# Sums of weight quarters: on VectorE, or by accumulating transfers

## The chip, the cores and the metric

The kernel runs on one core of a Trainium2 chip. A core has TensorE (matrix products into PSUM banks), VectorE and ScalarE (elementwise work), GpSimd (POOL in the profile) and SyncE (SP), each an engine with an in-order queue of its own, and 16 DMA engines that they share. The metric is the device time of one execution in microseconds: less is better.

## The reference

One inference step of a decoder of two layers, for a prompt of 1024 tokens and 8 single sample tokens, which the kernel handles together as 1032 columns. Layer 0 mixes tokens by a gated linear recurrence, layer 1 by a wide causal convolution. In both, a cross-attention over 256 memory tokens and then a gated feed-forward block follow. Only the last is touched:

```
gu = h @ ffn_w_up[i]                 # (1032, 1024) @ (1024, 6144)
g, u = gu[..., :3072], gu[..., 3072:]
g = causal depthwise convolution of width 3 over g (+ bias)
out = (gelu(g) * u) @ ffn_w_down[i]
```

All of it is float32.

## The kernel before, in words

*Precision.* Every operand of a matmul is split in a high part h, rounded by ScalarE (`act`), and a low part l, the rest, subtracted by VectorE. A product is three passes: hh, hl, lh.

*The up projection, seven products for eight.* The 24 gate tiles of 128 outputs and the 24 value tiles are taken in pairs p. Of a pair, the weights are two tiles of 128 x 8 x 128 (one of the gate, one of the value), each in two halves of the contraction: four quarters A11, A12 (gate), A21, A22 (value) of 128 x 512 floats. The activations are also cut in four (two halves of the contraction, two halves of the columns). A product of 2 x 2 blocks takes eight block products; the kernel uses the scheme of Strassen and Winograd with seven, P1 to P7, whose operands are sums and differences of the quarters. `QP` says for each product which of three PSUM accumulators (a, b, c) it goes into and which activation operand (b11, b21, b22, t1 to t4) it uses; `QFIRST`, `qsequence` and `QLAST` write out the order of the 168 products of a layer, in the middle P1, P6, P2, P7, P5, P4, P3 of one pair after the other.

*Weights.* Three products use a quarter as it is (P1: A11, P2: A12, P4: A22). The other four use sums, which class `QWeights` (from L587) makes on VectorE in tiles `ws`: (1) A21 + A22, (2) that minus A11, (3) A11 - A21, (4) A12 minus sum 2. `high` and `low` split the result in `wh` and `wl`. The two tiles of a pair are loaded whole, 512 KB each, by SP through `load_raw` into a ring of three buffers `w`; `fetch` issues the next load once all readers of the oldest tile stand in the program.

*The loop over products* (in `ffn`, from L1267). In iteration i TensorE runs product i (`qprod`, L521: four k-blocks, three passes, two chunks of 258 columns, 24 matmuls), then the program gives ScalarE `high(i + 5)` and VectorE `low(i + 4)`, the next steps of the convolution of earlier pairs (`conv`; one of them is a GpSimd copy of the last columns of g into `fstash`), the evacuation of product i (`evac`), the weight sums that a table `wsums` puts in this iteration, and what `beside` adds for the activations of the first nine iterations. Products that share an accumulator wait for the evacuation between them: P1 is copied out of a (tile e) before P2 is added in it, P6 out of b (tile g) before P7, P7 (tile u) before P4, P5 out of c before P3. Iterations 7, 9 and 10 hold the three parts of the row norms (`Rms`: matmuls with ones, a square root on ScalarE, a reciprocal on VectorE).

*Before the loop* the output projection of the attention (`out_proj`, from L826) makes eight output tiles of 72 matmuls each, and behind each of them parts of the first operands: at its tiles 5 and 6 the first four sums and the first weight splits. Tile 7 is computed before tile 6 is worked on. It reloads x from DRAM through SP and spills it through ScalarE's queue.

*After the loop* `close` releases the loads of the down projection, which uses the same ring `w` and DRAM copies `ad` of the gated activations.

Of the kernel before, what the change touches and what calls it, by code (L numbers as in the profile page):

```python
# [15 lines left out]
P = 128  # L16
D = 1024
KD = 8
# [29 lines left out]
NPART = 3  # L48
LOOK = 2
RAHEAD = 1  # L50


@with_exitstack
def hybrid_step(
# [70 lines left out]
    def f32(ap):  # L125
        return ap.bitcast(F32)
# [60 lines left out]
                w_cols((nme, l, m), w[l, 0, m])  # L187

    def w_ffn(l):
        for t in range(24):  # L190
            w_cols(("up", l, t), w_up[l, 0, t])
            w_cols(("up", l, 24 + t), w_up[l, 0, 24 + t])
        for gi in range(24 // GS):
            for m2 in range(4):
                w_cols(("dn", l, gi, m2), w_down[l, gi, m2], GS, 256)
# [36 lines left out]
    def prep(n):  # L232

        while wstate["made"] < min(wstate["cur"] + n, wstate["lim"]):
            i = wstate["made"]
            load_raw(i + 1 + RAHEAD)
            w = W(order[i][1])
            for j in range(2):
                act(w.h[j], wraw[i][:, j * w.n:(j + 1) * w.n])
            wmade.append(w)  # L240
            wstate["made"] += 1
        prep_low(n)
# [14 lines left out]
        wstate["cur"] += 1  # L257
        return wmade[i]

    limits = [i for i, o in enumerate(order) if o[0][0:1] == ("up",) and order[i - 1][0][0] == "o"]  # L260
    wstate["lim"] = limits.pop(0)


# [265 lines left out]
    class Quarters:  # L529
# [13 lines left out]
        def sum(self, n, i):  # L543

            y, t = self.y, self.t
            a, b, into = {"t1": (y.get((i, 1)), y.get((i, 0)), None),
                          "t2": (y.get((i + 2, 1)), t.get(("t1", i)), t.get(("t1", i))),
                          "t3": (y.get((i + 2, 1)), y.get((i, 1)), y.get((i, 1))),
                          "t4": (y.get((i + 2, 0)), t.get(("t2", i)), y.get((i + 2, 0)))}[n]
            t[(n, i)] = slot(n, [P, 2, HT]) if into is None else into  # L550
            tt(V, t[(n, i)], a, b, ALU.subtract)
# [5 lines left out]
        def high(self, n, i):  # L557
            h = self.ops[n][0]
            h[i] = slot(n + "h", [P, 2, HT], F32R)
            act(h[i], self.src(n, i))  # L560

        def low(self, n, i):
            h, l = self.ops[n]
            l[i] = slot(n + "l", [P, 2, HT], F32R)
            tt(V, l[i], self.src(n, i), f32(h[i]), ALU.subtract)

        def split(self, n, i):
            self.high(n, i)
# [18 lines left out]
    class QWeights:  # L587


        SUM = {"P5": 1, "P6": 2, "P7": 3, "P3": 4}  # L590

        def __init__(self, pairs, seq):
            self.pairs, self.seq = pairs, seq
            self.sums, self.made, self.slots = {}, {}, {}

        def start(self, base):
            self.base = base
            for p, (k0, k1) in enumerate(self.pairs):
                assert (order[base + 2 * p][0], order[base + 2 * p + 1][0]) == (k0, k1)

            self.left = {base + 2 * p + i: 7 - 2 * i for p in range(len(self.pairs)) for i in range(2)}
            self.done = base

        def fetch(self):

            while self.left.get(self.done) == 0:
                self.done += 1
            load_raw(min(self.done + NRAW, self.base + 2 * len(self.pairs)))

        def raw(self, p, i, half):  # L610
            n = self.base + 2 * p + i
            load_raw(n + 1)
            self.left[n] -= 1
            assert self.left[n] >= 0
            return wraw[n][:, 4 * half:4 * half + 4, :]

        def sum(self, p, n):
            if (p, n) in self.sums or p >= len(self.pairs):
                return
            half = (p, n > 2)  # L620
            if half not in self.slots:
                self.slots[half] = slot("ws", [P, 2, 4, P])
            t = self.slots[half][:, (n - 1) % 2]
            op = ALU.subtract
            if n == 1:
                a, b, op = self.raw(p, 1, 0), self.raw(p, 1, 1), ALU.add
            elif n == 2:
                a, b = self.sums[(p, 1)], self.raw(p, 0, 0)
            elif n == 3:
                a, b = self.raw(p, 0, 0), self.raw(p, 1, 0)  # L630
            else:
                a, b = self.raw(p, 0, 1), self.sums[(p, 2)]
            self.sums[(p, n)] = t
            tt(V, t, a, b, op)

        def src(self, n):
            p, name = self.seq[n]
            if name in self.SUM:
                return self.sums[(p, self.SUM[name])]
            return self.raw(p, *{"P1": (0, 0), "P2": (0, 1), "P4": (1, 1)}[name])  # L640

        def high(self, n):
            if n < len(self.seq):
# [7 lines left out]
                tt(V, w[1], self.src(n), f32(w[0]), ALU.subtract)  # L651

        def close(self):
            n = 2 * len(self.pairs)
            for key in ("cur", "made", "low"):
                wstate[key] = self.base + n
            wmade.extend([None] * (self.base + n - len(wmade)))
            wstate["lim"] = len(order) if not limits else limits.pop(0)

    st = {}  # L660
# [165 lines left out]
    def out_proj(key, ops, g, src, dst, done=(), hooks={}, pair=None, quarters=None, qw=None):  # L826
# [13 lines left out]
        for m in range(KD):  # L840
            if m < len(done) and done[m] is not None:
                ps = done[m]
            else:
                ps = mmt()
                step(ps, getw(key + (m,)), ops, hooks.get(m))
            xm = xs[m]
            tt(V, v3(xm), ps[:, :, 0:CH], v3(xm), ALU.add)
            if quarters:
                quarters.tile(m, xm, g(m))
                norm_tile(st, m, xm, None, m > 5)  # L850
            else:
                xg.append(norm_tile(st, m, xm, g(m)))
            spill(dst, m, xm)
            if m + 2 < KD:
                xs.append(reload(src, m + 2))
            if not quarters:
                continue
            if m in (1, 3):
                quarters.sum("t1", m // 2)
                quarters.high("b11", m // 2)  # L860
            if m in (2, 4):
                quarters.low("b11", m // 2 - 1)
                quarters.split("t1", m // 2 - 1)
            if m == 5:
                qw.fetch()
                for n in range(1, 5):
                    qw.sum(0, n)
                qw.high(0)
                qw.low(0)
                quarters.sum("t2", 0)  # L870
                quarters.split("b21", 0)
            if m == 6:

                late = mmt()
                step(late, getw(key + (7,)), ops, hooks.get(7))
                done = [None] * 7 + [late]
                for n in range(1, 4):
                    qw.high(n)
                    qw.low(n)
                qw.fetch()  # L880
                quarters.high("t2", 0)
            if m == 7:
                quarters.low("t2", 0)
                quarters.sum("t2", 1)
                quarters.split("b21", 1)
# [21 lines left out]
        G.dma_start(out=o_lru_conv_s[0, :, 0:2, :], in_=state_lru_conv[0, :, 1:3, :])  # L907


    up_w = [QWeights([(("up", l, t), ("up", l, 24 + t)) for t in range(24)], qsequence(24)) for l in range(2)]  # L910
    pm = const([P, 2, NS, 32], "pm")
    G.memset(pm, 0.0)

    def attention(l, st, xg, g_next, src, dst, hooks=None):
        qw = up_w[l]
        qw.start(wstate["cur"] + 2 * KD)
        qd = dram([NS, NH, HD], f"qd{l}")
        od = dram([4, P, NP], f"od{l}")
        q, q8, o = {}, {}, {}
# [347 lines left out]
    def ffn(l, st, q, g_next, src, dst, hooks={}):  # L1267
# [12 lines left out]
        def evac(p, n):  # L1280
# [5 lines left out]
            elif n == "P6":  # L1286
                if p not in gs:
                    gs[p] = slot("g")
                tt(V, hv(gs[p][:, hi]), ps, hv(es[p]), ALU.add)
            elif n == "P2":  # L1290
                if p not in gs:
                    gs[p] = slot("g")
                act(hv(gs[p][:, lo]), ps)
            elif n == "P7":
                us[p] = slot("u")
                tt(V, hv(us[p][:, hi]), ps, hv(es[p]), ALU.add)
                if p in left:
                    left.pop(p)()
            elif n == "P5":
# [4 lines left out]
                else:  # L1304
                    left[p] = fin
            elif n == "P4":
                tt(V, hv(us[p][:, lo]), ps, hv(es.pop(p)), ALU.add)
            elif n == "P3":
                tt(V, hv(gs[p][:, hi]), ps, hv(gs[p][:, hi]), ALU.add)

        whole = {p: i for i, (p, n) in enumerate(seq) if n == "P3"}

# [35 lines left out]
        def a_parts(t):  # L1348
            parts[t] = parts_of("act", raw.pop(t))


        wsums = {0: [(1, 1), (1, 2)], 2: [(1, 3)], 4: [(1, 4)], 9: [(2, 1), (2, 2)], 11: [(2, 3)], 13: [(2, 4)]}
        for i, (p, n) in enumerate(seq):
            if p > 1 and i > 14 and n in ("P2", "P7", "P5"):
                if p == npair - 2:
                    wsums[i - 1 if n == "P2" else i] = {"P2": [(p + 1, 1)], "P7": [(p + 1, 2)], "P5": [(p + 1, 3)]}[n]
                    wsums[i + 1] = [(p + 1, 4)] if n == "P5" else []
                    continue
                wsums[i] = {"P2": [(p + 1, 1), (p + 1, 2)], "P7": [(p + 1, 3)], "P5": [(p + 1, 4)]}[n]
        r = Rms(st["acc"], *st["late"])  # L1360
        PART = {7: 0, 9: 1, 10: 2}
        end = len(seq) - len(QP)
# [1 line left out]
        for i, (p, n) in enumerate(seq):  # L1364
# [22 lines left out]
            conv(i)  # L1387
            if s <= 3:
                evac(p, n)
            for k in wsums.get(i, ()):  # L1390
                qw.sum(*k)
            qw.fetch()
            for f, *at in beside.get(i, ()):
                f(*at)
        use_banks("mm")
# [449 lines left out]
```

## Time and profile before

| | |
|---|---|
| median of 3 runs | 2850.26 us (2848.57 to 2850.32) |
| the profiled execution, whole | 2849.45 us |
| its span in the trace | 2847.3 us |
| TensorE busy | 2799.0 us (98%), 19814 matmuls |
| VectorE busy | 1887.3 us (66%) |
| ScalarE busy | 1082.9 us (38%) |
| GpSimd busy | 95.8 us (3%) |
| DMA: SP's queue, ScalarE's, GpSimd's | 249.45, 52.82 and 19.07 MB |
| HBM read, written | 255.25 and 67.23 MB |

The two up projections lie about from 645 to 1138 us and from 2061 to 2554 us. The granted clock of TensorE is at its full level nearly throughout (0.998 on the mean). A busy share says how long an engine had work; whether that work decides the time is read from who waits for whom.

### The profile page before, as it was taken

To read this page: it belongs to the slowest core of one execution; us is meant where nothing else is said; L and a number is where in the kernel's file an instruction comes from. 1 tells how busy PE (TensorE), PEld (TensorE's weight loads), DVE (VectorE), ACT (ScalarE), POOL (GpSimd) and SP (SyncE) were. 2 spreads that over 40 slices of the span, in tenths; PEclk is the share of its full clock that TensorE was granted. 3 is DMA by queue.
4 is the path that set the end of the run, shared out by engine and by line. 5 is a ranking of instruction groups with operands and counts; after the bars stand their busy time and mean duration, and the time that the engine had idled before them with its cause. 6 is when DMAs were issued, how large, how long until landed. Compare 5 with 4: busy or idle time off the path is not lost.

```text
span 2847.3 us, 46857 instructions
## 1 busy us (share of the span) xinstructions
PE 2799.0 (98%) x19814; PEld 2701.6 (95%) x19814; DVE 1887.3 (66%) x2673; ACT 1082.9 (38%) x1608; POOL 95.8 (3%) x175
## 2 busy tenths in 40 slices
PE   8999999999999999999999999999999999999998
PEld 6999999899999999999999679998999999999997
DVE  7686445658777777436688975456587777773456
ACT  7465333444333334322321154333453333343223
POOL 1000000000000000000000100000000000000001
PEclk9999999999999999999999999999999999999999
DMA  8111425732222223333312644267322222233231
GB/s 292 49 45 52 142 82 198 260 115 67 83 75 83 76 82 108 124 123 136 116 45 81 152 134 178 90 222 237 117 69 69 90 69 88 74 137 111 90 136 60
DMA packets 128529, 324.32 MB, mean 114 GB/s; under 512 B 17523, under 2 KB 61619, under 8 KB 128280
## 3 DMA queue, kind: packets, MB, share of 16 engines
q1 hardware_dynamic: 100976, 249.45, 27.0%
q10 hardware_dynamic: 15696, 52.82, 4.6%
q0 software_dynamic: 11648, 19.07, 2.5%
q8 instruction: 155, 2.54, 0.4%
q14 instruction: 54, 0.44, 0.0%
HBM read 255.25 MB, written 67.23 MB: 113 GB/s over the span
## 4 chain that ended last, share of the span: by engine, by line
PE 90%; DVE 4%; DMA 2%; ACT 2%; issue 1%; POOLq 0%; POOL 0%; ACTq 0%; DVEq 0%; SPq 0%
PE mm L277 48%; PE qm L521 33%; PE aux L1628 2%; PE mm L374 2%; PE aux L942 1%; DMA qb<-qd 1%; PE aux L985 1%; PE mm L1505 1%; PE aux L1505 1%; DMA w<-in_w_kv_dram 1%; DVE kc L120 1%; PE aux L461 1%; PE aux L1067 0%; DVE wl L117 0%; DVE qf L117 0%
## 5 line engine op out<-in xcount | busy, mean ns | idle before, releaser
L114 ACT ACTIVATE wh<-w 128x512 fp32r<-128x512 f32 x468 | 279.9, 624 | 461.5 <-PE mm L277 294.5
L117 DVE TENSOR_TENSOR wl<-w,wh 128x512 fp32r<-128x512 f32 x468 | 306.1, 686 | 106.4 <-ACT wh L114 106.4
L277 PE MATMUL mm<-xgh,wh 128*128 128x344 f32 x1152 | 249.0, 324 | 2.0 <-DVE qf L117 2.0
L277 PE MATMUL mm<-xgh,wl 128*128 128x344 f32 x1152 | 244.1, 320 | 0.0
L277 PE MATMUL mm<-xgl,wh 128*128 128x344 f32 x1152 | 244.1, 320 | 0.0
L277 PE MATMUL mm<-acth,wh 128*128 128x344 f32 x1056 | 223.8, 320 | 0.0
L277 PE MATMUL mm<-acth,wl 128*128 128x344 f32 x1056 | 223.8, 320 | 0.0
L277 PE MATMUL mm<-actl,wh 128*128 128x344 f32 x1056 | 223.8, 320 | 0.0
L277 PEld LDWEIGHTS mm<-xgh,wh 128*128 128x128 f32 x1152 | 190.8, 188 | 8.3 <-issue 3.3
L277 PEld LDWEIGHTS mm<-xgh,wl 128*128 128x128 f32 x1152 | 193.6, 188 | 0.0
L277 PEld LDWEIGHTS mm<-xgl,wh 128*128 128x128 f32 x1152 | 193.2, 188 | 0.0
L114 ACT ACTIVATE wh<-ws 128x512 fp32r<-128x512 f32 x192 | 120.8, 629 | 164.1 <-PE qm L521 133.4
L117 DVE TENSOR_TENSOR z<-mm,z 128x1032 f32<-128x1032 f32 x64 | 78.8, 1232 | 152.6 <-PE mm L277 152.6
L277 PEld LDWEIGHTS mm<-acth,wl 128*128 128x128 f32 x1056 | 177.6, 188 | 0.0
L277 PEld LDWEIGHTS mm<-actl,wh 128*128 128x128 f32 x1056 | 177.0, 188 | 0.0
L277 PEld LDWEIGHTS mm<-acth,wh 128*128 128x128 f32 x1056 | 176.7, 188 | 0.1
L120 DVE SCALAR_TENSOR_TENSOR dc<-glu,colB,dc 128x1015 f32<-128x1015 f32 (+29 forms) x120 | 145.9, 1265 | 0.7
L117 DVE TENSOR_TENSOR wl<-ws,wh 128x512 fp32r<-128x512 f32 x192 | 131.2, 684 | 7.7 <-ACT wh L114 7.7
L120 DVE SCALAR_TENSOR_TENSOR c<-g,colB,c 128x1023 f32<-128x1023 f32 x96 | 122.8, 1279 | 0.0
L117 DVE TENSOR_TENSOR x<-mm,x 128x1032 f32<-128x1032 f32 x40 | 49.3, 1232 | 108.4 <-PE mm L277 108.4
L117 DVE TENSOR_TENSOR acc<-acc,sq 128x1032 f32<-128x1032 f32 (+3 forms) x59 | 60.0, 1017 | 73.7 <-ACT sq L114 73.4
L117 DVE TENSOR_TENSOR g<-qm,e 128x516 f32<-128x516 f32 x48 | 33.4, 695 | 113.3 <-PE qm L521 113.3
(347 smaller groups left out, 6657.6 us busy)
## 6 DMA issues: line engine op xcount, KB each, us to landing
w<-in_w_up_dram SPq DMA_DIRECT2D x96, 512.0 KB, 3.6
ad<-u ACTq DMA_DIRECT2D x48, 516.0 KB, 2.7
ar<-ad SPq DMA_DIRECT2D x48, 516.0 KB, 4.7
w<-in_w_down_dram SPq DMA_DIRECT2D x48, 512.0 KB, 3.7
xd<-x ACTq DMA_DIRECT2D x40, 516.0 KB, 2.7
x<-xd SPq DMA_DIRECT2D x40, 516.0 KB, 5.4
w<-in_w_kv_dram SPq DMA_DIRECT2D x32, 512.0 KB, 5.1
kc<-in_cache_mem_k_dram SPq DMA_DIRECT2D x32, 512.0 KB, 7.6
```

The lines of the kernel that those rows point to most:

```text
L114: return S.activation(out=out, in_=in_, func=func, **kw)
L117: return e.tensor_tensor(out=out, in0=a, in1=b, op=op)
L120: return V.scalar_tensor_tensor(out=out, in0=a, scalar=sc, in1=b, op0=op0, op1=op1, **kw)
L277: PE.matmul(ps[:, c, 0:CH], w[wi](k), xs[k][xi][:, c * CH:(c + 1) * CH], start=(k == first and n == 0), stop=(k == last and n == passes[-1]))
L374: PE.matmul(ps[:, t, :], kv.memg[k // 4][xi][:, k % 4, t * P:(t + 1) * P], w[wi](k % 2), start=(k == 0 and n == 0), stop=(k == KD - 1 and ...
L461: PE.matmul(out, ident[:, 32 * g:32 * g + 1].to_broadcast([P, P]), self.q, start=True, stop=True)
L521: PE.matmul(acc[:, c, 0:HC], w[wi][:, k, :], x[xi][k // 2][:, k % 2, c * HC:(c + 1) * HC], start=first and k == 0 and i == 0, stop=last an ...
L942: PE.matmul(a[:, t * 256:(t + 1) * 256], q[2 * self.h + d][qi][:, c0:c0 + P], self.kv[ki][:, d * 256:(d + 1) * 256], start=(d == 0 and n = ...
L985: PE.matmul(a, self.kv[vi][:, c0:c0 + P], self.PT[hf][pi][:, mc, :], start=(mc == 0 and n == 0), stop=(mc == 1 and n == len(PASSES) - 1))
L1505: PE.matmul(ps[:, 0:n], w[m // 2][wi](k)[:, (m % 2) * P:(m % 2 + 1) * P], a[k][xi][:, r], start=(k == 0 and i == 0), stop=(k == GS - 1 and ...
L1628: PE.matmul(a[32 * g:32 * g + 32, lo:512], tap_w[j][:, 4 * q + g, :], tap_x[j][g][:, s0:s0 + 512 - lo], start=(q == 0), stop=(q == 7), til ...
```

## The change

Each product's weights now get a tile of their own, filled by transfers from DRAM: the first quarter plain from SP, each further quarter by a transfer from GpSimd that adds to what lies there (`accum_op`). `PARTS` lists the quarters of each product, 14 per pair, seven plain and seven added. Since only additions are made, the weight sums of P3, P6 (and P4's use of e) come with other signs than before: `t3` and `b22` are negated on the activations' side, P4, P6, P7 and P3 are evacuated with subtractions whose operands are swapped or whose operation changes. The four sums on VectorE, `fetch`, `raw` and the table `wsums` go, and the up weights leave the list `order` of whole tiles. `todo` gives part r of product n the iteration n - 7 - 2 x (parts - 1 - r), so that the last part is issued seven products ahead and parts lie two products apart; `go(i)` issues what is due, at the end of iteration i, and at output tiles 4, 5 and 6 before the loop. A tile holds two products; odd ones come from the general slots `ws`, the others from the ring `w`. `load_raw` in `prep` no longer reads past the limit.

```diff
+QAHEAD = 7
@@ w_ffn
-        for t in range(24):
-            w_cols(("up", l, t), w_up[l, 0, t])
-            w_cols(("up", l, 24 + t), w_up[l, 0, 24 + t])
@@ prep
-            load_raw(i + 1 + RAHEAD)
+            load_raw(min(i + 1 + RAHEAD, wstate["lim"]))
@@ Quarters
-                          "t3": (y.get((i + 2, 1)), y.get((i, 1)), y.get((i, 1))),
+                          "t3": (y.get((i, 1)), y.get((i + 2, 1)), y.get((i, 1))),
...
-            act(h[i], self.src(n, i))
+            act(h[i], self.src(n, i), **({"scale": -1.0} if n == "b22" else {}))
...
-            tt(V, l[i], self.src(n, i), f32(h[i]), ALU.subtract)
+            if n == "b22":
+                stt(l[i], self.src(n, i), -1.0, f32(h[i]), ALU.mult, ALU.subtract)
+            else:
+                tt(V, l[i], self.src(n, i), f32(h[i]), ALU.subtract)
@@ QWeights
-            if n == 1:
-                a, b, op = self.raw(p, 1, 0), self.raw(p, 1, 1), ALU.add
-            elif n == 2:
-                a, b = self.sums[(p, 1)], self.raw(p, 0, 0)
-            elif n == 3:
-                a, b = self.raw(p, 0, 0), self.raw(p, 1, 0)
-            else:
-                a, b = self.raw(p, 0, 1), self.sums[(p, 2)]
-            self.sums[(p, n)] = t
-            tt(V, t, a, b, op)
+        PARTS = {"P1": ((0, 0),), "P2": ((0, 1),), "P4": ((1, 1),), "P5": ((1, 0), (1, 1)),
+                 "P7": ((0, 0), (1, 0)), "P6": ((0, 0), (1, 0), (1, 1)),
+                 "P3": ((0, 0), (1, 0), (1, 1), (0, 1))}
+            self.todo = sorted((n - QAHEAD - 2 * (len(self.PARTS[name]) - 1 - r), n, r)
+                               for n, (p, name) in enumerate(seq) for r in range(len(self.PARTS[name])))
+        def go(self, i):
+            while self.todo and self.todo[0][0] <= i:
+                _, n, r = self.todo.pop(0)
+                p, name = self.seq[n]
+                j = n // 2
+                if j not in self.tiles:
+                    if j > 2 and j % 2:
+                        self.tiles[j] = slot("ws", [P, 2, 4, P])
+                    else:
+                        self.tiles[j] = wp.tile([P, 2, 4, P], F32, tag="w", name=nm("w"), bufs=NRAW)
+                q = self.quarter(p, *self.PARTS[name][r])
+                if r == 0:
+                    nc.sync.dma_start(out=self.src(n), in_=q)
+                else:
+                    G.dma_start(out=self.src(n), in_=q, accum_op=ALU.add)
@@ out_proj
+            if m == 4:
+                qw.go(-6)
             if m == 5:
-                qw.fetch()
-                for n in range(1, 5):
-                    qw.sum(0, n)
+                qw.go(-3)
...
-                qw.fetch()
+                qw.go(-1)
@@ evac
-                tt(V, hv(gs[p][:, hi]), ps, hv(es[p]), ALU.add)
+                tt(V, hv(gs[p][:, hi]), hv(es[p]), ps, ALU.subtract)
...
-                tt(V, hv(us[p][:, hi]), ps, hv(es[p]), ALU.add)
+                tt(V, hv(us[p][:, hi]), ps, hv(es[p]), ALU.subtract)
...
-                tt(V, hv(us[p][:, lo]), ps, hv(es.pop(p)), ALU.add)
+                tt(V, hv(us[p][:, lo]), ps, hv(es.pop(p)), ALU.subtract)
...
-                tt(V, hv(gs[p][:, hi]), ps, hv(gs[p][:, hi]), ALU.add)
+                tt(V, hv(gs[p][:, hi]), hv(gs[p][:, hi]), ps, ALU.subtract)
@@ the loop over products
-        wsums = {0: [(1, 1), (1, 2)], 2: [(1, 3)], 4: [(1, 4)], 9: [(2, 1), (2, 2)], 11: [(2, 3)], 13: [(2, 4)]}
...
-            for k in wsums.get(i, ()):
-                qw.sum(*k)
-            qw.fetch()
+            qw.go(i)
```

The order of instructions on the engines moves at three places. First, VectorE at the entry of the first up projection, from the last operand b21 of the output projection on (t2l, t3l: low parts of activations, y: an activation difference, wl: low part of a weight, ws: a weight sum). Before:

```order
528 L117 TENSOR_TENSOR b21l_5985<-y_5878,b21h_5983 128x1032
529 L117 TENSOR_TENSOR wl_5992<-w_5787,wh_5991 128x512
530 L117 TENSOR_TENSOR ws_6025<-w_5970 128x512
531 L117 TENSOR_TENSOR ws_6025<-ws_6025,w_5787 128x512
532 L117 TENSOR_TENSOR t2l_6030<-t_798_5589,t2h_6028 128x1032
533 L117 TENSOR_TENSOR y_5339<-y_5679,y_5339 128x1032
534 L117 TENSOR_TENSOR wl_6020<-ws_5789,wh_6019 128x512
```

And now:

```order
524 L118 TENSOR_TENSOR b21l_5993<-y_5882,b21h_5991 128x1032
525 L118 TENSOR_TENSOR wl_6000<-w_5697,wh_5999 128x512
526 L118 TENSOR_TENSOR t2l_6036<-t_798_5589,t2h_6034 128x1032
527 L118 TENSOR_TENSOR y_5339<-y_5339,y_5679 128x1032
528 L118 TENSOR_TENSOR wl_6028<-w_5697,wh_6027 128x512
```

The two sums between the weight's low part and t2l are gone, and the difference y has its operands swapped.

Second, GpSimd in the middle of the up projection. Before, there is nothing but a copy to `fstash` per pair:

```order
60 L1320 COPY fstash<-g_10231 128x10
61 L1320 COPY fstash<-g_10460 128x10
62 L1320 COPY fstash<-g_10689 128x10
63 L1320 COPY fstash<-g_10918 128x10
64 L1320 COPY fstash<-g_11148 128x10
```

And now, over one pair (the names are the tiles: ws_9061 and ws_9298 hold a P6, w_9159 the P3, w_9196 the P7, ws_9229 the P5):

```order
130 L617 DMA ws_9061<-in_w_up_dram 128x512
131 L1296 COPY fstash<-g_8957 128x10
132 L617 DMA ws_9061<-in_w_up_dram 128x512
133 L617 DMA w_9159<-in_w_up_dram 128x512
134 L617 DMA w_9196<-in_w_up_dram 128x512
135 L617 DMA ws_9229<-in_w_up_dram 128x512
136 L617 DMA w_9159<-in_w_up_dram 128x512 x2
137 L617 DMA ws_9298<-in_w_up_dram 128x512
138 L1296 COPY fstash<-g_9193 128x10
139 L617 DMA ws_9298<-in_w_up_dram 128x512
```

Seven accumulating transfers now stand between two copies, each behind the landing of the transfer before it on the same tile: the two of row 136 wait for row 133 and for each other, row 139 for row 137.

Third, SP in the same stage. Before, it holds whole tiles, two per pair:

```order
150 L228 DMA w_6798<-in_w_up_dram 128x1024
151 L228 DMA w_6929<-in_w_up_dram 128x1024
152 L228 DMA w_7027<-in_w_up_dram 128x1024
153 L228 DMA w_7158<-in_w_up_dram 128x1024
154 L228 DMA w_7256<-in_w_up_dram 128x1024
```

And now quarters, seven per pair:

```order
229 L615 DMA ws_8960<-in_w_up_dram 128x512
230 L615 DMA ws_9061<-in_w_up_dram 128x512
231 L615 DMA w_8923<-in_w_up_dram 128x512
232 L615 DMA ws_9061<-in_w_up_dram 128x512
233 L615 DMA w_9159<-in_w_up_dram 128x512
234 L615 DMA w_9196<-in_w_up_dram 128x512 x2
235 L615 DMA ws_9229<-in_w_up_dram 128x512
```

Each of these is a first quarter; the tile's further quarters are GpSimd's. TensorE's order is the same in both kernels.

## Rows read from the trace of the kernel before

**Rows 1.** The page's first lines: busy us, share of the span, instructions.

```profile
span 2847.3 us, 46857 instructions
PE 2799.0 (98%) x19814; PEld 2701.6 (95%) x19814; DVE 1887.3 (66%) x2673; ACT 1082.9 (38%) x1608; POOL 95.8 (3%) x175
```

**Rows 2.** Stretches: us, busy PE, PEld, DVE, ACT, POOL, clock, DMA share, GB/s.

```profile
0.00:20.00 20.00, 13.40 (x49) 10.77 (x50) 13.13 (x22) 14.14 (x25) 1.82 (x11) 1.00 0.86 306
690.00:1130.00 440.00, 440.00 (x3655) 440.00 (x3653) 327.85 (x461) 168.09 (x241) 12.59 (x22) 1.00 0.25 85
2105.00:2545.00 440.00, 440.00 (x3654) 440.00 (x3653) 328.48 (x461) 168.14 (x241) 12.57 (x22) 1.00 0.25 85
```

**Rows 3.** The chain that ended last: start us, us, what.

```profile
584.31 61.09 PE mm L277 x387
...
683.58 448.15 PE qm L521 x3720
```

**Rows 4.** What TensorE waited for: us in total, times, longest us.

```profile
PE qm L521 <- DVE u L117: 5.3, 4, 1.9
...
PE qm L521 <- ACT e L114: 1.3, 2, 0.7
```

**Rows 5.** TensorE in order of time, layer 0: start us, us, ..., [idle before <-releaser].

```profile
657.60 0.51 PE L521 MATMUL qm<-b21h,wh 128*128 128x258 f32 x2 [0.65 <-ACT e L114]
675.83 0.48 PE L521 MATMUL qm<-t4h,wh 128*128 128x258 f32 x2 [1.87 <-DVE u L117]
...
1132.50 0.51 PE L521 MATMUL qm<-t4h,wh 128*128 128x258 f32 x2 [0.79 <-DVE u L117]
```

**Rows 6.** The tile ws, two of the four sums: ns min/median/max, first and last.

```profile
L117 DVE TENSOR_TENSOR ws<-ws,w x48: 681/692/695, 628.2 to 2525.2; 128x512 f32<-128x512 f32 x48
...
L117 DVE TENSOR_TENSOR ws<-w,ws x48: 680/682/693, 629.4 to 2531.1; 128x512 f32<-128x512 f32 x48
```

**Rows 7.** VectorE, then ScalarE, in order of time at the entry.

```profile
651.74 0.69 DVE L117 TENSOR_TENSOR ws<-w 128x512 f32<-128x512 f32 x1
652.46 0.69 DVE L117 TENSOR_TENSOR ws<-ws,w 128x512 f32<-128x512 f32 x1
653.07 1.23 DVE L117 TENSOR_TENSOR t2l<-t,t2h 128x1032 fp32r<-128x1032 f32 x1
...
655.47 1.07 ACT L114 ACTIVATE t3h<-y 128x1032 fp32r<-128x1032 f32 x1 [1.65 <-DVE y L117]
```

**Rows 8.** The chain at the norm's first part: start us, us, what.

```profile
669.42 0.97 PE aux L447 x13
670.40 0.57 issue
670.97 1.28 ACT L114
...
672.26 0.49 ACT rq L114
...
672.77 1.77 DVE rq L453
```

**Rows 9.** The page's costliest groups: a scalar_tensor_tensor of VectorE, busy us, mean ns.

```profile
L120 DVE SCALAR_TENSOR_TENSOR dc<-glu,colB,dc 128x1015 f32<-128x1015 f32 (+29 forms) x120 | 145.9, 1265 | 0.7
```

**Rows 10.** DMA from 690 to 1130 us: queues (packets, MB, share); an issue.

```profile
q1 hardware_dynamic: 6900, 25.15, 18.2%
q10 hardware_dynamic: 3168, 11.63, 6.5%
...
w<-in_w_up_dram SPq DMA_DIRECT2D x41, 512.0 KB, 3.6
```

**Rows 11.** GpSimd's transfers by line (L384 kvtok, L403 KT) and tx: landing.

```profile
DMA to landing us min/median/max: 3.0/6.7/8.6
...
L403 POOL DMA_DIRECT2D kvd<-KT x4: 727/733/738, 50.1 to 1704.3; - x4
...
DMA to landing us min/median/max: 3.8/5.2/6.7
...
tx<-gd POOLq DMA_DIRECT2D x16, 516.0 KB, 16.8
```

More of the change, by code (lines that the diff above doesn't have):

```diff
@@ L258, in getw @@
         return wmade[i]
-    limits = [i for i, o in enumerate(order) if o[0][0:1] == ("up",) and order[i - 1][0][0] == "o"]
+    limits = [i for i, o in enumerate(order) if o[0][0:1] == ("dn",) and order[i - 1][0][0] == "o"]
     wstate["lim"] = limits.pop(0)
@@ L587, in hybrid_step @@
     class QWeights:
[L590 to L624, printed above, removed]
-            if n == 1:
-                a, b, op = self.raw(p, 1, 0), self.raw(p, 1, 1), ALU.add
-            elif n == 2:
-                a, b = self.sums[(p, 1)], self.raw(p, 0, 0)
-            elif n == 3:
-                a, b = self.raw(p, 0, 0), self.raw(p, 1, 0)
-            else:
-                a, b = self.raw(p, 0, 1), self.sums[(p, 2)]
-            self.sums[(p, n)] = t
-            tt(V, t, a, b, op)
+        PARTS = {"P1": ((0, 0),), "P2": ((0, 1),), "P4": ((1, 1),), "P5": ((1, 0), (1, 1)),
+                 "P7": ((0, 0), (1, 0)), "P6": ((0, 0), (1, 0), (1, 1)),
+                 "P3": ((0, 0), (1, 0), (1, 1), (0, 1))}
@@ new lines, in __init__ @@
+        def __init__(self, quarter, seq):
+            self.quarter, self.seq = quarter, seq
+            self.made, self.tiles = {}, {}
+            self.todo = sorted((n - QAHEAD - 2 * (len(self.PARTS[name]) - 1 - r), n, r)
[15 more added lines that the diff above has]
+                    G.dma_start(out=self.src(n), in_=q, accum_op=ALU.add)
@@ L636, in src @@
         def src(self, n):
[L637 to L640, printed above, removed]
+            return self.tiles[n // 2][:, n % 2]
         def high(self, n):
@@ L653, in close @@
         def close(self):
[L654 to L657, printed above, removed]
             wstate["lim"] = len(order) if not limits else limits.pop(0)
@@ L907, in lru_states @@
         G.dma_start(out=o_lru_conv_s[0, :, 0:2, :], in_=state_lru_conv[0, :, 1:3, :])
-    up_w = [QWeights([(("up", l, t), ("up", l, 24 + t)) for t in range(24)], qsequence(24)) for l in range(2)]
+    up_w = [QWeights(lambda p, i, half, l=l: w_up[l, 0, 24 * i + p][:, 4 * half:4 * half + 4, :], qsequence(24))
+            for l in range(2)]
     pm = const([P, 2, NS, 32], "pm")
@@ L915, in attention @@
         qw = up_w[l]
-        qw.start(wstate["cur"] + 2 * KD)
         qd = dram([NS, NH, HD], f"qd{l}")
@@ L1349, in a_parts @@
             parts[t] = parts_of("act", raw.pop(t))
-        wsums = {0: [(1, 1), (1, 2)], 2: [(1, 3)], 4: [(1, 4)], 9: [(2, 1), (2, 2)], 11: [(2, 3)], 13: [(2, 4)]}
[L1353 to L1359, printed above, removed]
         r = Rms(st["acc"], *st["late"])
```

## The prediction

> **What bounds the kernel now.** I read the page's first section, then the idle time of TensorE by stage, then the chain of waits at the seams of the stage that changes. TensorE is busy for 2799.0 of 2847.3 us; VectorE, which the change relieves, for 1887.3 [rows 1]. So all that any relief of VectorE can win lies in 48.3 us of TensorE idle time. By stage it is smaller still: from 690 to 1130 us, inside the first up projection, TensorE is busy 440.00 of 440.00 us, and the same in the second (2105 to 2545), with VectorE at 327.85 us (75%) [rows 2]. The chain says the same: one unbroken piece of 448.15 us in 3720 matmuls [rows 3], so 24 matmuls of one product take 2.89 us and the seven products of a pair 20.24 us. In this stage nothing waits for VectorE; it waits for TensorE.
>
> The idle time is at the seams. Over the whole span the products (qm, L521) waited for VectorE four times, 5.3 us together, and for ScalarE twice, 1.3 us [rows 4]: per layer 0.65 us, 1.87 us and 0.79 us [rows 5]. These 6.6 us are the ceiling of what the change could give back, if it does no harm.
>
> **The change part by part.** My unit is the profiled execution: 2849.45 us, that is the span of 2847.3 and 2.15 around it; the median of the runs shown, 2850.26, is 0.81 above it.
>
> *Removed: 192 sums on VectorE*, 48 of each of four kinds; of the two kinds shown one takes 692 ns and the other 682 in the median [rows 6]. At 0.686 in the middle that is 131.7 us. What covers them now is TensorE: in the full stretch they cost nothing, and taking them away gives nothing there. At the entry two of them lie in the chain [rows 7]: VectorE starts them at 651.74 and 652.46 and is free for t2l at 653.07, 1.33 us after the first began; behind t2l comes y, ScalarE stands 1.65 us for y before t3h, then does wh and e, and TensorE stands 0.65 us for e at 657.60. Without the two sums this chain is 1.33 us earlier, and 0.65 is less than 1.33, so the stall goes; what is late next is product 3 itself, TensorE's own work. Gain 0.65 x 2 layers = 1.3 us. The 1.87 us stall stays: its chain starts on TensorE (stats, end 670.40) and goes through ScalarE's table load 1.28, the root 0.49 and VectorE's reciprocal 1.77 [rows 8] to one rounding and u, for which TensorE waits [rows 5]; no sum is in it. The 0.79 us at the end stays too: there u evacuates P7, which must be done before P4 goes into the same bank.
>
> *Signs.* The swapped operands of g and u change neither count nor size. The two b22 lows per layer become scalar_tensor_tensor: 1.27 us for 1015 columns [rows 9] against 1.23 us for a subtract of 1032 like t2l [rows 7], four times 0.05 us, beside full TensorE work: nothing. If ScalarE's negated copy took longer than a plain one, the first lies before the table load, in front of which ScalarE is idle for 0.57 us.
>
> *Moved to the DMA engines.* A pair needs 14 quarters of 128 x 512 floats, 0.262 MB each: seven plain from SP, seven accumulating from POOL. In all that is 336 and 336, or 88.1 MB each, for 96 loads of 50.3 MB. In the 440 us stretch, 21.74 pairs, it is 39.9 MB plain and 39.9 MB accumulating. There SP's queue now moves 25.15 MB in 18.2% of the 16 engines' time, 0.724% per MB, and ScalarE's 11.63 MB in 6.5% [rows 10]. Of SP's bytes 41 loads of 0.524 MB [rows 10] go, 3.7 MB remain, so plain traffic takes 43.6 x 0.724 + 6.5 = 38.0%, and accumulating traffic 28.9% times k, where k is its cost against a plain byte. No row shows an accumulating transfer. From below k = 1, as many bytes land (66.9% in all); I exclude less, since it reads a destination as well. From above, the farthest rows: tx, 516 KB from POOL, lands in 16.8 us and kvd<-KT, 512 KB from POOL, in 5.2 [rows 11], k = 3.2 (130%). I take k between 1.5 and 2 (81 to 96%), nearest to the lower end: it fits, with little room. The engines have been as full before: 0.86 and 306 GB/s in the first 20 us [rows 2].
>
> The Trainium skill, "Collectives: The Full Stack", section "The bandwidth ceiling: the fold count and why AG ≠ RS ≠ AR", says that an add in the DMA path costs no cycles but needs two source reads on one ring, and measured a ratio of 1.93. By it k would be about 2 and the stretch 95.8% full, still inside; no run here shows it yet. It is the rule that speaks most against this change, and the reason why rival C keeps its chance.
>
> *The new wait.* Each accumulation must wait until the transfer before it on the same tile has landed, and POOL is in order: what stands behind a waiting accumulation is every later one, and the fstash copy that frees a g tile. In POOL's new order, per pair: P6's last part, P3a, P7, P5, P3b, P3c, P6a, fstash. P3b waits for P3a's landing, P3c for P3b's, the next P6b for P6a's: three landings in series per 20.24 us, so the queue keeps up while a landing L is under 6.75 us. Bounds for L: plain 512 KB loads from SP in this very stage land in 3.6 us [rows 10]; 512 KB stores from POOL in 3.0 to 8.6 us, median 6.7, and kvd<-KT in 3.8 to 6.7, median 5.2; tx in 16.8 [rows 11]. An accumulation of 256 KB reads 512 KB, so I take kvd<-KT, 5.2 us: 15.6 of 20.24 us, and it hides. POOL's own issue, 0.73 us at kvd<-KT [rows 11], would be 5.1 us for seven, and part of it lies inside L. The last part of a product is issued seven products (20 us) before TensorE needs it, two (5.8 us) before ScalarE wants to round it; if it is a little late ScalarE and VectorE wait, but the products' banks allow only one product (2.89 us) before an evacuation is missed. SP's seven plain loads wait for buffers last read three products earlier, so they don't queue up.
>
> *Entry.* The loads of the first P1 and P5 are issued after the fifth output tile of the attention's projection; P1 is rounded one tile later and P5 two. A tile is 72 matmuls of the 387 in 61.09 us [rows 3], 11.4 us, more than two landings of 5.2; nothing is late.
>
> Sum: 2849.45 - 1.3 = 2848.2 for such an execution, 2850.26 - 1.3 = 2849.0 for the median.
>
> **Rivals.**
> A, the forecast: hidden traffic, 0.65 us per layer won. 2849.0, own range 2845 to 2855.
> B, slower: POOL's serial landings. If L averages above 6.75 us, each us above costs 3 us per pair, over some 46 pairs 138 us per us: at 8.6 us 2850 + 255 = 3105; at the far end, 16.8, about 4240; just past the limit, at 7.0, 2885. For it: a median of 6.7 among POOL's stores, with the bus at two to three times its load. Against: half the bytes, and an idle POOL (12.59 us of 440 [rows 2]).
> C, slower: the DMA engines become the bound. It decides at k = 62.0/28.9 = 2.15. At k = 2.5 the stage needs 110%: 0.10 x 20.24 x 48 = 99 us more, 2949; at 3.2, 130%, 3145. For it: the narrow room. Against: the stretch from 0 to 20 us.
> D, faster: with VectorE from 75% to 61% in the stage all three seam stalls go, 2 x 3.3 = 6.6 us: 2843.6. Against: the chain of rows 8 holds no sum.
> E, slightly slower: the first pair's accumulations come late at the entry, where reloads of x share SP's queue; one landing of 5.2 us per layer: 2860.
> F: the change does nothing at all, since the 0.65 us hang on product 3 and not on the sums: 2850.3, inside A's range.
>
> **How the numbers follow.** A and F 62%, B 18%, C 10%, E 5%, D 5%. A difference under 0.2% (5.7 us) is about what a measurement of this kernel can't tell from none. A and F lie within it, D just beyond, B, C and E beyond it on the other side: faster 0.05, same 0.62, slower 0.33. The range: below, 2845 leaves out D; above, B and C spread from 2856 to over 3100, and to leave out some 15% I go to 2905 (L about 7.15 us, or k about 2.3).
>
> **What would show it.** VectorE's total falls by 131.7 to about 1756 us and the sums' rows are gone; TensorE's matmul count is the same and it stays at 440 of 440 us inside the stage; the wait of qm for e is gone, those for u stay. POOL's queue moves 88.1 MB more and SP's 37.8 more; the DMA share in the stretch is 0.67 to 0.96. Landing of the accumulating quarters under 6.75 us confirms the step on POOL; TensorE waiting for wh or wl (or for e, g, u all through the stage) would refute it, and then the landing time tells B (long, with engines not full) from C (share near 1). The forecast is wrong if TensorE idles periodically, once per 20 us, between 690 and 1130.

## The result, and the profile after

The changed kernel takes 2896.85 us (median of 4 runs, 2896.51 to 2905.74) against 2850.29 us before (4 runs): 1.0171 times as long, 95% interval 1.0159 to 1.0183. It is slower by 46.6 us, where no change (2849.0) was forecast. The profiled execution took 2905.74 us, the longest of the four; its span is 2904.0, 56.7 us more than before, and what is read below is this execution's loss.

The page's first lines, the answer to [rows 1]:

```profile
span 2904.0 us, 48024 instructions
PE 2816.6 (97%) x19814; PEld 2707.0 (93%) x19814; DVE 1778.8 (61%) x2481; ACT 1071.1 (37%) x1608; POOL 376.8 (13%) x511
```

VectorE's total fell by 108.5 us with 192 instructions fewer, TensorE has the same 19814 matmuls, and GpSimd has gone from 95.8 to 376.8 us. The stage tells more. These are stretches of the first up projection after the change (columns as in [rows 2]):

```profile
690.00:735.00 45.00, 45.00 (x375) 45.00 (x375) 31.13 (x42) 18.47 (x26) 14.39 (x18) 1.00 0.87 202
735.00:1105.00 370.00, 360.08 (x2957) 357.44 (x2956) 219.89 (x297) 128.26 (x194) 111.67 (x140) 1.00 0.88 200
```

Until 735 us TensorE is unbroken as before; then 9.9 of 370 us are missing. Where the time goes is best seen by following one instruction of each pair, ScalarE's evacuation e of P1, through both traces of layer 0:

| e of the ... pair | 2nd | 8th | 16th | 23rd | 24th |
|---|---|---|---|---|---|
| before, us | 657.0 | 796.4 | 958.3 | 1100.0 | 1123.1 |
| after, us | 656.3 | 795.3 | 964.6 | 1112.9 | 1149.1 |
| later by | -0.7 | -1.0 | 6.3 | 13.0 | 26.0 |

The entry is won, by somewhat more than forecast; from the ninth pair on the kernel falls behind step by step, and at the last pair by 13 us at once. Layer 1 repeats it (from 26.0 to 46.4 at the 23rd pair and 56.9 at the 24th).

Who waits in the middle of the stage (us in total, times, longest): three lines from before, 690 to 1130 us, then 735 to 1105 us now, first ScalarE, then GpSimd:

```profile
POOL fstash L1320 <- DVE g L117: 421.3, 22, 19.8
ACT wh L114 <- PE qm L521: 116.5, 65, 2.3
ACT wh L114 <- DVE ws L117: 11.4, 22, 2.1
...
ACT wh L115 <- DMA ws<-in_w_up_dram: 105.7, 36, 7.9
ACT wh L115 <- DMA w<-in_w_up_dram: 100.7, 34, 7.3
...
POOL w L617 <- DMA w<-in_w_up_dram: 124.1, 24, 8.5
POOL ws L617 <- DMA ws<-in_w_up_dram: 108.2, 24, 6.2
POOL w L617 <- DMA ws<-in_w_up_dram: 18.0, 3, 6.6
```

Before, ScalarE's roundings waited here mostly for TensorE, a little for the sums, and never for a landing. Now they wait 206 us for landings, and GpSimd itself stands 250 us for landings and is busy for 112: it has no slack. No wait of `fstash` for VectorE appears in this answer, where it was GpSimd's main wait before. GpSimd's 51 waits are three per pair. By the order of the transfers each is behind GpSimd's own transfer before it on the same tile, and most end 0.28 us after that one's landing; so it is not SP's first quarters for which GpSimd stands, though the last line names another tile. The DMA queues and issues of the same stretch (packets, MB, share of 16 engines; KB each, us to landing) and the landing of GpSimd's accumulations, min/median/max:

```profile
q0 software_dynamic: 17594, 32.03, 54.6%
q1 hardware_dynamic: 17587, 32.02, 27.1%
q10 hardware_dynamic: 2545, 9.32, 6.2%
...
ws<-in_w_up_dram SPq DMA_DIRECT2D x61, 256.0 KB, 5.6
...
DMA to landing us min/median/max: 3.8/6.4/9.6
```

An accumulated byte takes 1.705% per MB against 0.846% for a plain one from SP, so k = 2.01. And an accumulation lands after 6.4 us, a plain quarter after 5.6, where plain loads of twice the size took 3.6 [rows 10].

GpSimd in order of time over one pair:

```profile
739.36 1.75 POOL L617 DMA_DIRECT2D w<-in_w_up_dram  x2 [4.64 <-DMA w<-in_w_up_dram]
740.47 2.41 POOL L617 DMA_DIRECT2D ws<-in_w_up_dram  x2
747.61 0.86 POOL L617 DMA_DIRECT2D w<-in_w_up_dram  x1 [4.73 <-DMA w<-in_w_up_dram]
752.83 0.86 POOL L617 DMA_DIRECT2D w<-in_w_up_dram  x1 [4.35 <-DMA w<-in_w_up_dram]
753.42 1.17 POOL L617 DMA_DIRECT2D ws<-in_w_up_dram  x1
754.40 0.59 POOL L1296 COPY fstash<-g 128x10 f32<-128x10 f32 x1
759.78 0.86 POOL L617 DMA_DIRECT2D ws<-in_w_up_dram  x1 [4.79 <-DMA ws<-in_w_up_dram]
```

These are the three links in series: P6b and P3a at 739.36, then P3b at 747.61, P3c (and P6a behind it) at 752.83, the next P6b at 759.78. From P6b to P6b it is 20.42 us here; over the stretch 123 accumulations, 17.57 pairs, in 370 us, 21.06 us per pair. TensorE wants 20.24.

The seam at the end of the layer: TensorE in order of time, pieces of the chain (start us, us, what), then two stretches (columns as in [rows 2]):

```profile
1149.71 0.58 PE L519 MATMUL qm<-b21h,wh 128*128 128x258 f32 x1 [6.81 <-ACT e L115]
...
1149.71 8.57 PE qm L519 x48
...
1159.05 6.04 PE qm L519 x48
...
1140.00:1150.00 10.00, 3.19 (x26) 2.98 (x25) 1.83 (x2) 3.54 (x5) 0.00 (x0) 0.76 0.71 238
1150.00:1160.00 10.00, 9.21 (x55) 9.01 (x55) 5.97 (x8) 5.57 (x9) 0.00 (x0) 0.73 0.00 0
```

ScalarE had stood 10.79 us for the last weights of the last pair (P3, in a tile ws), with e queued behind; TensorE stood 6.81 us for e. The 48 matmuls after the pause took 8.57 us, those after them 6.04: the granted clock was 0.76 in the stretch 1140 to 1150, in which TensorE was busy for 3.19 us, 0.73 in the next ten, and 1.00 from 1160 to 1170. So the pause cost some 2.5 us more in matmuls of which a part ran at 1.2 instead of 2.4 GHz. A shorter fall lies ahead of it, 0.92 from 1130 to 1140 us with TensorE busy throughout, behind a pause of 2.23 us that ended at 1126.67.

### The profile page after: what moved, and what is told of

The parts are those of the page before. It is cut to its first block, busy times and chain, and to the rows that moved or that the text cites. A ratio compares the mean times of both kernels' runs of the same rounds, so it can differ in the third digit from the quotient of the medians.

```text
span 2904.0 us, 48024 instructions
## 1 busy us (share of the span) xinstructions
PE 2816.6 (97%) x19814; PEld 2707.0 (93%) x19814; DVE 1778.8 (61%) x2481; ACT 1071.1 (37%) x1608; POOL 376.8 (13%) x511
## 4 chain that ended last, share of the span: by engine, by line
PE 63%; DMA 15%; issue 12%; DVE 5%; POOL 3%; ACT 2%; SPq 0%; POOLq 0%; ACTq 0%; DVEq 0%
PE mm L275 47%; PE qm L519 9%; DMA w<-in_w_up_dram 5%; DMA ws<-in_w_up_dram 5%; PE aux L918 1%; DMA qb<-qd 1%; DMA ad<-u 1%; PE mm L372 1%; POOL ws L617 1%; DMA tx<-gd 1%; POOL w L617 1%; PE aux L1593 1%; PE aux L961 1%; DVE kc L121 1%; DMA w<-in_w_kv_dram 1%
## 5 line engine op out<-in xcount | busy, mean ns | idle before, releaser
L115 ACT ACTIVATE wh<-w 128x512 fp32r<-128x512 f32 x496 | 295.8, 624 | 605.3 <-PE mm L275 293.6
L118 DVE TENSOR_TENSOR wl<-w,wh 128x512 fp32r<-128x512 f32 x496 | 325.6, 686 | 214.3 <-ACT wh L115 214.1
L617 POOL DMA_DIRECT2D w<-in_w_up_dram x162 | 171.6, 1179 | 471.4 <-DMA w<-in_w_up_dram 327.5
L617 POOL DMA_DIRECT2D ws<-in_w_up_dram x174 | 179.0, 1153 | 399.1 <-DMA ws<-in_w_up_dram 374.6
L115 ACT ACTIVATE wh<-ws 128x512 fp32r<-128x512 f32 x164 | 101.8, 626 | 250.7 <-DMA ws<-in_w_up_dram 239.1
L118 DVE TENSOR_TENSOR wl<-ws,wh 128x512 fp32r<-128x512 f32 x164 | 112.7, 687 | 97.0 <-ACT wh L115 96.7
```

What stands on the lines that cost most here:

```text
L115: return S.activation(out=out, in_=in_, func=func, **kw)
L118: return e.tensor_tensor(out=out, in0=a, in1=b, op=op)
L617: G.dma_start(out=self.src(n), in_=q, accum_op=ALU.add)
```

## The experiments

Theory 1: GpSimd's queue holds three landings in series per pair, and three are too long. Rivals: the DMA engines' throughput (2), SP's plain loads late behind buffers (3), too short a lead (4). All kernels below are edits of the changed one.

**P6's parts three products apart** (e1):

```diff
-            self.todo = sorted((n - QAHEAD - 2 * (len(self.PARTS[name]) - 1 - r), n, r)
+            self.todo = sorted((n - QAHEAD - (3 if name == "P6" else 2) * (len(self.PARTS[name]) - 1 - r), n, r)
```

> The parts of P6 lie three products apart instead of two, nothing else: the same transfers, bytes and sums, but on GpSimd P6a now stands ahead of P3c and its landing runs beside P3b's, so a pair has two landings in series instead of three. Theory 1 (GpSimd's serial landings set the pace: 3 x about 6.4 us plus the issues is more than 20.24 us): two landings, about 14 us, fit; the loss is gone, 2848 to 2855 us, TensorE without gaps from 735 to 1125 us. Theory 2 (the DMA engines, 0.88 full, set the pace, whatever the order): no change, about 2897. Theory 3 (plain loads come late because SP stands before a buffer): no change or slightly worse, 2897 to 2905, since P6's tiles live longer.

Measured: 2845.88 us, 0.9974 of before (0.9965 to 0.9984). The same bytes and sums, and not only is the loss gone, it is faster than before. The same stretch, the queues, the landing, and GpSimd over one pair:

```profile
735.00:1105.00 370.00, 370.00 (x3071) 370.00 (x3070) 227.33 (x311) 139.41 (x202) 124.05 (x149) 1.00 0.92 210
...
q0 software_dynamic: 18482, 33.67, 55.5%
q1 hardware_dynamic: 18448, 33.62, 29.6%
...
DMA to landing us min/median/max: 3.7/6.7/9.8
...
815.94 0.59 POOL L1296 COPY fstash<-g 128x10 f32<-128x10 f32 x1 [6.30 <-DVE g L118]
816.48 1.74 POOL L617 DMA_DIRECT2D w<-in_w_up_dram  x2
817.55 2.45 POOL L617 DMA_DIRECT2D ws<-in_w_up_dram  x2
824.46 0.86 POOL L617 DMA_DIRECT2D w<-in_w_up_dram  x1 [4.47 <-DMA w<-in_w_up_dram]
825.00 1.22 POOL L617 DMA_DIRECT2D ws<-in_w_up_dram  x1
830.66 0.86 POOL L617 DMA_DIRECT2D w<-in_w_up_dram  x1 [4.44 <-DMA w<-in_w_up_dram]
836.20 0.59 POOL L1296 COPY fstash<-g 128x10 f32<-128x10 f32 x1 [4.68 <-DVE g L118]
```

Two waits for landings are left, and then GpSimd stands at `fstash` for VectorE: it is ahead of TensorE again. Landings are not shorter (6.7 us), and the engines are fuller (0.92). So neither throughput nor the landing alone was the bound; the number of landings in series was. Theories 2 and 3 fall.

**The same transfers without the addition** (e2), which leaves the weight sums out:

```diff
-                    G.dma_start(out=self.src(n), in_=q, accum_op=ALU.add)
+                    G.dma_start(out=self.src(n), in_=q)
```

> The further quarters are sent by GpSimd in the same order, with the same waits and sizes, but overwrite the tile instead of being added to it, so the sums are left out. Theories 1 and 2: a byte then costs as in a plain load (half of the share measured for an accumulated byte), the share falls from 0.88 to about 0.6, the landing from 6.4 to about 5 us or less, three of them fit and the loss is gone: 2848 to 2852. Theory 3: the same number of transfers and of buffer waits, so most of the loss stays, 2885 to 2897.

Measured: 2848.21 us, 0.9988 (0.9978 to 0.9998). The share is 0.64 in the stretch, its queues

```profile
q1 hardware_dynamic: 18432, 33.83, 28.8%
q0 software_dynamic: 10391, 34.07, 28.1%
```

cost the same per byte (0.97), GpSimd's landing is 4.0 us in the median of all, and an issue on GpSimd lasts 0.54 us where it lasted 0.86. Three links of 4.0 us fit in 20.24 us. The addition is thus what makes a link too long; transfers, buffers and waits alone are harmless. Whether it does so by a landing that is longer in itself or by the engines that it fills, this run doesn't separate.

**A lead of nine** (e3, `QAHEAD = 9`):

> QAHEAD 9 instead of 7: every part is issued two products (5.8 us) earlier, order and bytes unchanged. Theories 1 and 2 (a pace below TensorE's): the loss per pair, about 1 us, is the same, only the first 5.8 us per layer are taken up by the lead: 2880 to 2890. Theory 4 (the pace is enough and only the lead of seven products is too short for single late landings): the loss goes, 2848 to 2855.

Measured: 2911.58 us, 1.0208 (1.0193 to 1.0223). All the theories missed: an earlier issue made it worse by 15 us, so theory 4 falls too. The landing is as long as with a lead of seven (6.5 us), and SP's queue stands no longer before its loads (309 of 370 us; 307 in the changed kernel). In the traces the difference arises in layer 0, where the 23rd pair is 22.9 us late (13.0 in the changed kernel); layer 1 adds 18.8 (20.4). Why the longer lead costs more there, the runs don't show.

**P3's weights by one sum on VectorE** (e4), from P6's tile and P2's quarter, ten quarters per pair:

```diff
-                 "P3": ((0, 0), (1, 0), (1, 1), (0, 1))}
+                 "P3": ()}
...
+            for n, a, b in self.p3.pop(i, ()):
+                self.tile(n // 2)
+                tt(V, self.src(n), self.src(a), self.src(b), ALU.add)
```

> The weights of P3 are made by one VectorE sum per pair from the finished tile of P6 and the quarter of P2, instead of by one plain and three accumulating transfers: 10 quarters per pair (6 plain, 4 accumulating), 48 sums of 0.69 us back on VectorE, and GpSimd's chain of P3 is gone (one landing in series per pair). Theories 1 and 2: the share falls to about 0.57, nothing is late: 2847 to 2850. Theory 3: also about 2850, since six loads instead of seven wait for buffers. If VectorE mattered in the stage, it would be slower than that.

Measured: 2850.87 us, 0.9993 (0.9984 to 1.0003), share 0.64 where 0.57 was expected. The loss is gone, as all three theories had it, but nothing tells the kernel from the one before; it is some 5 us behind e1, which the trace does not explain. One thing in it matters for what follows, GpSimd's accumulations from 735 to 1105 us (KB each, us to landing):

```profile
ws<-in_w_up_dram POOLq DMA_DIRECT2D x39, 256.0 KB, 7.4
...
w<-in_w_up_dram POOLq DMA_DIRECT2D x36, 256.0 KB, 7.5
```

They land later than in the changed kernel (6.4), though the engines are emptier on the mean (0.64 against 0.88). Up to four of them are issued here right behind each other.

**The other order among parts of one iteration** (e5), leads and tiles unchanged:

```diff
+            self.todo.sort(key=lambda t: (t[0], -t[1], t[2]))
```

> Leads, bytes and tiles as in the changed kernel; only parts due in the same iteration are issued in the other order, so GpSimd gets P3b before P5 and P6a before P3c: P6a's landing runs beside P3b's, two landings in series per pair. Theory 1 (serial landings): loss gone, 2845 to 2852, as in the run with P6 three apart. Theory 5 (there it was the two products of extra lead for P6's first two parts that helped): no change, about 2897.

Measured: 2847.97 us, 0.9988 (0.9979 to 0.9997). The stage, then GpSimd's waits from 735 to 1105 us:

```profile
735.00:1105.00 370.00, 370.00 (x3068) 370.00 (x3068) 228.08 (x311) 139.05 (x203) 122.38 (x147) 1.00 0.91 211
...
POOL fstash L1297 <- DVE g L118: 112.0, 19, 6.9
POOL w L618 <- DMA w<-in_w_up_dram: 76.8, 20, 6.4
POOL ws L618 <- DMA ws<-in_w_up_dram: 58.5, 16, 5.3
```

On GpSimd two neighbours per pair have changed places (P3b now ahead of P5, P6a ahead of P3c), on SP two as well. The 36 waits for landings are two per pair, GpSimd stands at `fstash` for VectorE again, and the whole loss is gone without any longer lead. So the extra lead of e1 was not needed (theory 5 falls).

**One more landing in series** (e6), by a copy of a column behind P3's last part:

```diff
                     G.dma_start(out=self.src(n), in_=q, accum_op=ALU.add)
+                    if name == "P3" and r == 3:
+                        G.tensor_copy(landed, self.src(n)[:, 0, 0:1])
```

> The changed kernel plus one copy of one column on GpSimd behind P3's last part, which makes GpSimd wait for that landing before it issues P6a: four landings in series per pair instead of three, no bytes added. Theory 1: 4 x (6.4 + about 0.5) = 27.6 us per pair against 20.24, some 7 us times 46 pairs less what the emptier DMA engines give back in landing time: 3050 to 3200. Theory 2 (DMA engines' throughput): no change, 2897 to 2905.

Measured: 3016.67 us (2 runs), 1.0578 (1.0557 to 1.06). It is slower by 120 us than the changed kernel, less than expected: the engines are emptier (0.79) and a landing is shorter, 5.7 us. GpSimd's landing and one pair, in order of time:

```profile
DMA to landing us min/median/max: 3.5/5.7/9.3
...
817.42 0.87 POOL L618 DMA_DIRECT2D w<-in_w_up_dram  x1 [0.33 <-issue]
817.97 0.52 POOL L1299 COPY fstash<-g 128x10 f32<-128x10 f32 x1
821.96 0.86 POOL L618 DMA_DIRECT2D w<-in_w_up_dram  x1 [3.46 <-DMA w<-in_w_up_dram]
...
829.44 0.86 POOL L618 DMA_DIRECT2D ws<-in_w_up_dram  x1 [3.94 <-DMA ws<-in_w_up_dram]
834.96 0.87 POOL L618 DMA_DIRECT2D ws<-in_w_up_dram  x1 [4.66 <-DMA ws<-in_w_up_dram]
839.74 0.19 POOL L620 COPY landed<-ws 128x1 f32<-128x1 f32 x1 [3.91 <-DMA ws<-in_w_up_dram]
```

Four waits per pair, 106 accumulations in 370 us, 24.4 us per pair: 6.1 us per link. With three links it was 21.06, 7.0 per link.

**The same copy on e1** (e7), three in series again:

> The kernel with P6's parts three apart (two landings in series, no loss) plus the same waiting copy: three in series again, the issue order otherwise unchanged. Theory 1: the loss comes back, about the changed kernel's time, 2880 to 2920. Theories 2 and 5: stays at 2846.

Measured: 2863.25 us (8 runs, 2849.13 to 2880.47), 1.0051 (1.0028 to 1.0073). A loss returns, but a small one, below what was expected: it is 17 us behind e1, where the changed kernel is 51 behind. In the trace TensorE loses 5.0 of 370 us from 735 to 1105, and nothing from 2200 to 2500 in layer 1. So three links stand here at the edge of 20.24 us, and one layer of the same run falls behind where the other does not. Why three links cost less here than in the changed kernel (other neighbours in the queue, and P6's earlier parts) the runs don't separate.

**A lead of nine with the other order** (e8):

> QAHEAD 9 with the other order among parts of one iteration: two landings in series, all parts two products earlier. With lead 9 and three in series 2911.6 us were measured. Theory 1 with buffers only as its amplifier (late landings delay the lows, the lows free the buffers, SP's loads wait): without late landings nothing is delayed, 2845 to 2852. Theory 6 (lead 9 costs by itself since SP's loads stand before buffers that are read later than they are wanted): still a loss, 2860 to 2890.

Measured: 2846.13 us, 0.9979 (0.997 to 0.9989). With two links in series the lead of nine costs nothing, so e3's extra loss is not the lead's own (theory 6 falls). SP still waits long for buffers here, 208 us for wl between 735 and 1105, without harm.

**More rounds** of e1's kernel (e9) and e8's (e10):

> The kernel with P6's parts three apart once more, in more rounds: whether it beats the kernel before, and by how much. From the traces, the entry of each up projection is about 1.1 us earlier than before (first stall gone, second 1.9 to 1.4 us) and nothing is lost inside: 2.2 us under the kernel before. The earlier run gave 0.9974. Expected 0.997 to 0.9995.

> Lead 9 with the other order among parts of one iteration, in more rounds. The same gain at the entries, the same two landings in series: 0.997 to 0.9995, no difference from the kernel with P6 three apart that can be told.

Measured: 2844.95 us, 0.9984 (0.9975 to 0.9993), and 2844.39 us, 0.9977 (0.9968 to 0.9986). Both beat the kernel before, by 5.2 and 5.7 us, and cannot be told apart.

## Why the prediction was wrong

- *What bounds the kernel, and the ceiling of the gain*: right. Nothing was won inside the stage; the kernels without the loss win 5.2 and 5.7 us (e9, e10), under the 6.6 that the seams hold.
- *The entry*: right in place, a little small in size. TensorE in order of time in the changed kernel has one stall left there:

```profile
674.63 0.48 PE L519 MATMUL qm<-t4h,wh 128*128 128x258 f32 x2 [1.36 <-DVE u L118]
```

The stall of 0.65 us is gone, as worked out, and that of 1.87 [rows 5] has become 1.36, which was held to stay. Behind the last matmul of the norm part ScalarE's table load had come after 0.57 us [rows 8]; now it follows at once; why, the runs don't show. That is 1.16 us per layer, 2.3 of the 5 us or so that e9 and e10 win; the rest is not located.
- *What VectorE loses*: the forecast total of about 1756 us was not met, it is 1778.8. The sums are all gone: the lengths of VectorE's instructions add up to 2044.9 us before and 1913.0 now, 131.8 less, as worked out. But the page's total counts a stretch in which two neighbours overlap once, and so fell by 108.5 only. The two b22 lows took 1.22 us each, no longer than a subtract; the 1.27 of [rows 9] is a mean over 30 forms.
- *The DMA engines*: k was taken between 1.5 and 2 and is 2.01 (1.87 in e1). The Trainium skill, "Collectives: The Full Stack", section "The bandwidth ceiling: the fold count and why AG ≠ RS ≠ AR", puts the price of an add down to two source reads and measured a ratio of 1.93. The size agrees with 2.01 here, and e2's 0.97 ties it to the addition; that a second read is the reason, no run here shows. Rival C did not come: at a share of 0.92 the stage still runs unbroken (e1).
- *The new wait: the step that failed.* The queue, the three landings in series and the limit of 6.75 us were in the prediction, as rival B; but the landing was sized from kvd<-KT, "so I take kvd<-KT, 5.2 us: 15.6 of 20.24 us, and it hides". Two terms of that sum were too small. A landing took 6.4 us for 256 KB. And what GpSimd needs from one landing to the start of the next link, of which the prediction said "part of it lies inside L", was left out of the sum: a link takes 7.0 us (21.06 / 3), 0.6 us more than the landing. An estimate from these figures says that either alone would still have hidden: 3 x 6.4 = 19.2 us, 3 x (5.2 + 0.6) = 17.4 us, both under 20.24. So the sign given for the step was wrong too: 6.4 us lies under the limit of 6.75 and would have confirmed it, but the limit holds for landing and hand-over together.
- *Why the row misled*: not because it was measured with emptier engines. While the four kvd<-KT were on their way the share was 0.66 to 0.98, and e4 has 7.4 us at a mean of 0.64. But each kvd<-KT was issued alone. Four other stores of GpSimd in the trace before, issued from 62.4 us on some 0.6 us apart, landed after 6.8, 7.5, 8.0 and 9.9 us (the first and third are among the eight of 3.0 to 8.6 us in [rows 11]). In the changed kernel the median landing is 5.0, 6.5, 7.3 and 8.1 us for the first, second, third and fourth accumulation in such a row (735 to 1105 us). No run isolates this.
- *What it cost*: by B's own price 7.0 us gave 2885. In the traces the pace costs 14.0 us from the 8th to the 23rd pair of layer 0 and 20.4 in layer 1.
- *What B had not*: the seam at the end, about 13 us in layer 0 and 10.5 in layer 1. The last pair's P3 is late, ScalarE's rounding of it stands ahead of e, and the clock falls with the pause. And "SP's seven plain loads wait for buffers ..., so they don't queue up" did not hold: SP's queue stood 307 of 370 us before its loads. But it stood 296 us in e1 without harm, and that it cost time here is not shown. e3 against e8 shows that the longer lead is dear only where three landings stand in series.
- *E, a late entry*: did not happen; the kernel was 1.0 us ahead at the 8th pair.

## What to carry to other kernels

Where a step in an in-order queue waits for the landing of an earlier one, count the landings that stand one behind the other in a period. Multiply by a landing measured for transfers that are issued as the change will issue them, several right behind each other, plus the time from a landing to the next start. The share of the DMA engines alone does not tell (0.88 lost 47 us, 0.92 none). If the product is near the period, change the order before the lead: the other order of the same issues (e5) took the whole loss away, two products more lead (e3) made it worse. Work taken off an engine that nobody waits for was worth no more here than what stood at the seams.

## What the runs showed of the hardware

An accumulating transfer from DRAM into SBUF took twice the DMA engines' time of a plain one of the same bytes (2.01, in e1 1.87; the same transfers without the addition 0.97), and its issue on GpSimd 0.86 instead of 0.54 us. With the engines at 0.88 to 0.92, 256 KB took 6.4 to 6.7 us to land; at 0.64 it took 4.0 us without the addition (e2) and 7.4 to 7.5 us with it, up to four in a row (e4). After a TensorE pause of 6.81 us, in a stretch in which it was busy for 3.19 of 10 us, the granted clock was 0.73 on the mean of the next 10 us and 1.00 in the 10 after.
